# Two blocks of mixers and routed experts on one core: the order of weight places, one more place, and matmuls of two row halves issued in turn

## The chip, the core and the metric

The kernel runs on one core of one Trainium2 chip. The metric is the time of one execution on the device in microseconds (us). Engines are named as in the profile: PE is TensorE's matmuls, PEld its weight loads, DVE is VectorE, ACT is ScalarE, POOL is GpSimd, SP is SyncE, whose queue issues nearly all the transfers.

## What is computed

256 tokens of width 1024 go through two layers of a first block and one layer of a second block, all in float32.

- A layer of the first block: RMS norm; a projection to queries, keys, values and gates; "dilated" attention (4 heads, each a mixture over strides 1, 4 and 16) beside windowed attention (16 query heads, 4 key heads, a sink logit); two branch projections, gated and summed; an output projection. Then expert-choice feed-forward: each of 16 experts takes its 32 best tokens, computes `silu(a) * u` with two 1024 x 1024 weights and goes through a third.
- The second block: sine positions, a modulated norm, and a token mixer of two branches. HGRN2 is a scan with a state per head, run in both directions in 8 chunks of 32 tokens, `S_new = exp(total) * S + (k * decay)^T v`; the Hyena branch is a long convolution by DFT. Then 32 experts in 4 groups (each token goes to 2), and a last norm.

All weights are read once, some 746 MB, in chunks of 128 partitions x 2048 float32 (1 MB).

## The kernel before, in words

**Places.** SBUF holds a chunk in a *place*. There are two kinds, 9 of tag "W" and 12 of tag "T" (`PLACES`, L297). The T places are also those of the large tiles: every tag in `WHOLE` (L294) is turned into "T" by `Core.t` (L75), so activations and weights share them. `Core.use` (L51) sets a ring of tags, as `ROOM` (L296), and `Core.chunk` (L60) takes the next tag of the ring, makes a tile of it and has `fetch` (L55) load it. `fetch` chains every load behind the one before on SP's queue, so the loads start in the order of the program, and one whose place is not yet free holds up all behind it. Smaller tags have slots of their own (`SMALL`, L299): "P" and "PT" four of 128 x 512 each, "wh" and "wl" three each for the two parts, a rounded one and the rest, into which `split` (L95) divides a weight for the projections (three matmuls per product, L121 to L123).

**Order of work.** `body` (L1549) writes the program in one line: mixer, experts, mixer, experts, token mixer, mixture of experts. Inside a stage generators are interleaved by `weave` (L313). A planner (`schedule_with_timeline_sim=True`) then sets the order on each engine and gives out the slots of each tag when the program is built; the engines run their instructions in that order.

**Experts of the first block.** `experts` (L717) routes the tokens, then takes the ring `ROOM` and asks for its 19 chunks ahead of the first matmul (L793, L794), then goes over to the ring "WT" in layer 0 (where the next layer's projections, `Ahead`, are woven into the second half) or `FEW` in layer 1 (L795). Expert by expert, eight chunks each, it multiplies (L810); the gather of the tokens (`gather_x`, L889) is interleaved with expert 0, and a second gather comes before expert 2. `gs` and `sg` are its work tiles (L818, tag "P"; L824, tag "PT"). The second half goes four experts at a time over the down weights (L863), q = 0 to 3. In layer 1 the filters and the context of the second block (`prep`) are interleaved.

**Attention.** `dilated_scores` (L439) computes for one pair of heads and one half of the tokens two banks of scores (tag "sc", 2 banks): first the three matmuls (L447) of the head in partitions 0 to 63, then those of the head in 64 to 127. Each half gets a tile P (tag "P") that is masked (L414), exponentiated (L417), scaled and transposed (L434).

**Scan.** In `hgrn` (L1166) each of the 8 steps multiplies the state (L1228); the update of the state goes direction by direction (L1232 to L1247): four matmuls over 32 partitions (L1238) into a bank, then four instructions on DVE (L1245) that make the next state.

**Other users of "P".** `rstd` (L163) squares into it; `ada_gate` (L621) loads a bias `gb` into it (L632, L633), in the token mixer just ahead of the load of the first `w2z` chunk, and in `moe` (L1348) just ahead of the first 16 chunks of the last stage (`ROOM2`, L1428, L1429); the token mixer's last addition uses it for `t1` (L1314).

**Last stage.** `moe` (L1329) asks for 16 chunks in the ring `ROOM2`, then uses "WWTWT"; `moe_quad` (L1470) takes four experts at a time.

Of the kernel before, what the change touches and what calls it, by code (L numbers as in the profile page):

```python
# [2 lines left out]

# [1 line left out]

# [4 lines left out]
F = mybir.dt.float32  # L10
# [3 lines left out]
OP = mybir.AluOpType  # L14
# [3 lines left out]
T, D = 256, 1024  # L18
# [4 lines left out]
PW = 2048  # L23
BIG = -1e33
HG = 4
# [7 lines left out]
class Core:  # L33
    def __init__(self, ctx, tc, A):
        self.tc, self.nc, self.A = tc, tc.nc, A
        self.const = ctx.enter_context(tc.tile_pool(name="const", bufs=1))
        self.sb = ctx.enter_context(tc.tile_pool(name="sb", bufs=1))
        self.ps = ctx.enter_context(tc.tile_pool(name="ps", bufs=1, space=PSUM))
        self.flip = self.nsplit = self.nchunk = 0

        self.share = 4
        self.after = nullcontext
        self.idle, self.pre, self.sent = (), [], None
        self.use("W")

    def load(self, name, shape, dt=F):
# [1 line left out]
        self.fetch(t, name)  # L48
        return t

    def use(self, places):  # L51

        self.ring = cycle(places)

    def fetch(self, out, src):  # L55

# [3 lines left out]
    def chunk(self, src, parts=1):  # L60

        tag = next(self.ring)
        t = self.sb.tile([128, PW], F, name="w", tag=tag, bufs=PLACES[tag])
        n = src.shape[1] // parts
        for i in range(parts):
            self.fetch(t[:, i * n:(i + 1) * n], src[:, i * n:(i + 1) * n])
        return t

    def next_chunk(self, src, parts=1):
        return self.pre.pop(0) if self.pre else self.chunk(src, parts)  # L70
# [3 lines left out]

    def t(self, shape, name, bufs=1, tag=None, dt=F):  # L75
        tag = tag or name
        if tag in WHOLE:
            tag, bufs = "T", PLACES["T"]
        return self.sb.tile(shape, dt, name=name, tag=tag, bufs=bufs)
# [122 lines left out]
class Quarters:  # L202

    shape = (128, PW)
# [87 lines left out]
HEAD = ((1, 3), (0, 3))  # L292

WHOLE = {"x", "hTa", "hTb", "qa", "qb", "qc", "V", "G", "hgw", "hn", "ob"}  # L294
ROOM2 = "TWWTTTTWWTTTWWWW"
ROOM, FEW = "TWWWWTTTTTTWWTTTWWW", "WWWWTWWWWWT"  # L296
PLACES = {"W": 9, "T": 12}  # L297
NP = 4
SMALL = {"P": NP, "PT": NP, "wh": 3, "wl": 3, "oa": 2}  # L299
BANKS = {"mm": 2, "sc": 2, "tp": 2, "acc": 2}  # L300
# [21 lines left out]

def mixer(K, h, l, ada, first=None, ahead=None):
    nc, A = K.nc, K.A
    if ahead:
        x = ahead.x
        ahead.turned(3)
    else:
        w_in = iter(A["w_in"])

        K.idle = range(K.nsplit + HEAD[l][0], K.nsplit + HEAD[l][1])
        x = K.pair("hT")
        K.transposed(h, lambda kb, p: K.split_to(x[0][:, kb, :], x[1][:, kb, :], p, K.gmix[:, l, kb:kb + 1]),
                     banks=("tp", "sc"))

    rs = K.rstd(h)
    p = K.bank("tp")
# [101 lines left out]
    def dilated_scores(pair, tt):  # L439
        q = slice(tt * 128, tt * 128 + 128)  # L440
        Ps, m, den = [], K.t([128, 2, 3], "m3", 2), K.t([128, 4], "den", 3)
        for half in range(2):
            s, hh = 2 * pair + half, slice(half * 64, half * 64 + 64)
            p = K.bank("sc")
            for g, (o, ks) in enumerate(((0, slice(0, 256)), (256, q), (384, q))):
                b = (4 * g + s) // 2
                nc.tensor.matmul(p[:, o:o + ks.stop - ks.start], lhsT=qd[b][hh, q], rhs=qd[6 + b][hh, ks],  # L447
                                 start=True, stop=True)
            P = K.t([128, 512], "P", NP)
            mh = m[:, half]  # L450
            ttr(P[:, :256], p[:, :256], K.negd[:, 512 + tt * 256:768 + tt * 256], SLOPE_A[s], 1e30, mh[:, 0:1])
            ttr(P[:, 256:384], p[:, 256:384], K.negd[:, 1024:1152], SLOPE_A[4 + s], mh[:, 0:1], mh[:, 1:2])
            ttr(P[:, 384:], p[:, 384:], K.negd[:, 1152:1280], SLOPE_A[8 + s], mh[:, 1:2], mh[:, 2:3])
            exponential(P, mh[:, 2:3], den[:, half:half + 1])
            Ps.append(P)
        r = K.t([128, 4], "r", 3)
        nc.vector.reciprocal(r[:, :2], den[:, :2])
        for half in range(2):
            nc.vector.tensor_scalar(Ps[half], Ps[half], r[:, half:half + 1], None, op0=OP.mult)
        return pair, tt, Ps  # L460
# [160 lines left out]
def ada_gate(K, g):  # L621

    nc = K.nc
    p = K.bank("acc")
    for c in range(4):
        w = K.chunk(K.A["ada"][2, 4 * g + c])
        with K.after():
            for j in range(4):
                nc.tensor.matmul(p[32 * j:32 * j + 32, :], lhsT=K.cs32[:, 2 * c + j // 2, :],
                                 rhs=w[:, j * 512:(j + 1) * 512], start=(c == 0), stop=(c == 3),  # L630
                                 tile_position=(0, 32 * j))
    gb = K.t([128, 512], "gb", NP, tag="P")  # L632
    K.fetch(gb, K.A["gtb"][g])  # L633
    K.ms = K.t([128, 512], "ms", tag="wr")
    nc.vector.tensor_add(K.ms, p, gb)
# [81 lines left out]
def experts(K, h, l, mix, ada, prep, ahead=None):  # L717
# [4 lines left out]
    next(rt)  # L722
    for _ in mix:
        next(rt)
    q = K.logits
    rs = K.rstd(h, dve=False, tag="oa")
    lg = K.t([128, 2, NE], "lg")
# [64 lines left out]

    K.use(ROOM)  # L793
    ws = [K.chunk(A["w_eg"][l, i // KD, i % KD]) for i in range(len(ROOM))]  # L794
    K.use("WT" if ahead else FEW)  # L795
    hid, Ge = [], []
    gw = K.t([128, 4], "gw4")
    for e in range(NE):
# [16 lines left out]
                pass  # L815
        if e % 8 == 0:
            hid.append(K.t([128, 8, 4, 64], "hid", tag=own[e // 8]))
        gs = K.t([128, 512], "gs", NP, tag="P")  # L818
        K.copy(gs, gu)
        p = K.bank("tp")  # L820
        for fb in range(4):
# [209 lines left out]

def token_mixer(K, h):
    nc, A, tc = K.nc, K.A, K.tc

    sc = K.t([128, 2, D], "sincos", tag="V")
    K.fetch(sc, "sincos")
# [129 lines left out]
    def hgrn():  # L1166
# [55 lines left out]
        for n in range(8):  # L1222

            for hd in range(HG):
                for d in range(2):
                    c = 7 - n if d else n
                    tt, cc = divmod(c, 4)
                    nc.tensor.matmul(oo[tt][32 * cc:32 * cc + 32, hd * 128:(hd + 1) * 128],  # L1228
                                     lhsT=steps[d][0][:, hd, c * 32:(c + 1) * 32], rhs=S[d][:, hd * 128:(hd + 1) * 128],
                                     start=False, stop=(n >= 4 and n % 4 == 3 and hd == HG - 1),  # L1230
                                     tile_position=(0, 32 * cc), skip_group_check=True)
            for d in range(2 if n < 7 else 0):  # L1232
                wk, b, kT, end = steps[d]
                c = 7 - n if d else n
                tt, cc = divmod(c, 4)
                u = K.bank("sc")
                for hd in range(HG):
                    nc.tensor.matmul(u[:, hd * 128:(hd + 1) * 128],  # L1238
                                     lhsT=kT[32 * cc:32 * cc + 32, tt, hd * 128:(hd + 1) * 128],
                                     rhs=v[32 * cc:32 * cc + 32, tt, hd * 128:(hd + 1) * 128], start=True, stop=True,  # L1240
                                     tile_position=(32 * cc, 0))
                S2 = K.t([128, 512], "PT", NP)
                for hd in range(HG):
                    sl = slice(hd * 128, (hd + 1) * 128)
                    nc.vector.scalar_tensor_tensor(S2[:, sl], S[d][:, sl], b[:, hd, c * 32 + end:c * 32 + end + 1],  # L1245
                                                   u[:, sl], op0=OP.mult, op1=OP.add)
                S[d] = S2  # L1247
            yield

    ya = K.t([128, 2, 4, T], "ya", tag="ob", dt=FR)  # L1250
# [78 lines left out]
def moe(K, h, mix):  # L1329
# [12 lines left out]
    next(rt)  # L1342
    for _ in mix:
        next(rt)
    q = K.logits
    rs = K.rstd(h, dve=False, tag="oa")
    K.after = lambda: tc.issue_after(K.routed.ins)
# [79 lines left out]

    K.use(ROOM2)  # L1428
    K.pre = [K.chunk(A["w2eg"][2 * i + x, c]) for i in range(2) for c in range(4) for x in range(2)]  # L1429
    K.use("WWTWT")  # L1430

    def gate(*args):
        spread_gate(*args)
# [36 lines left out]
def moe_quad(K, h, xT, oh, cmb, e, i, gate):  # L1470
# [45 lines left out]
    for hf in range(2):  # L1516
        sl = slice(hf * 512, (hf + 1) * 512)
        dn = K.bank("acc")
        end = e + 4 + hf == NE2 + 1

        wd = [K.next_chunk(A["w2ed"][e + x, hf], 4 if end and x == 3 else 1) for x in range(4)]
        for c in range(4):
            for x in range(4):
                nc.tensor.matmul(dn[32 * x:32 * x + 32, :], lhsT=hid[x][:, c, :], rhs=wd[x][:, c * 512:(c + 1) * 512],  # L1524
                                 start=(c == 0), stop=(c == 3), tile_position=(0, 32 * x))
        y = K.t([128, 512], "yt", NP, tag="P")
        nc.vector.scalar_tensor_tensor(y, dn, gw, K.gt[:, 1, sl], op0=OP.mult, op1=OP.mult)
        hi, lo = yd[:, 0, sl], yd[:, 1, sl]
        K.split_to(hi, lo, y)
        for tt in range(2):  # L1530
            p = K.bank("sc")
            for n, part_ in enumerate((hi, lo)):
                nc.tensor.matmul(p, lhsT=Ge[:, tt * 128:(tt + 1) * 128], rhs=part_, start=(n == 0), stop=(n == 1))
            hs = h[:, tt, sl]
            nc.vector.tensor_add(hs, p, hs)
# [214 lines left out]
```

## Time and profile before

| | us |
|---|---|
| median of 3 runs (2227.25 to 2230.5) | 2229.97 |
| the profiled execution, its own time | 2231.4 |
| its span, first to last instruction | 2229.6 |
| PE busy | 1803.5 (81%) |
| PEld busy | 1017.9 |
| DVE busy | 761.1 |
| ACT busy | 600.3 |
| POOL busy | 222.2 |

The transfers moved 748.83 MB, 336 GB/s over the span. Busy time is what an engine's instructions cover; an engine that waits is not busy. The stretch from 0 to about 275 us is the mixer of layer 0, to 785 its experts, to 965 the mixer of layer 1, to 1455 its experts, to 1755 the token mixer, to 2210 the last experts. The rows further down give for a stretch the busy time of each engine with the number of instructions in brackets, then the clock granted to TensorE as a share of 2.4 GHz, the share of time for which the DMA engines were busy, and GB/s.

### The profile page before, as it was taken

To read this page: it belongs to the slowest core of one execution; us is meant where nothing else is said; L and a number is where in the kernel's file an instruction comes from. 1 tells how busy PE (TensorE), PEld (TensorE's weight loads), DVE (VectorE), ACT (ScalarE), POOL (GpSimd) and SP (SyncE) were. 2 spreads that over 40 slices of the span, in tenths; PEclk is the share of its full clock that TensorE was granted. 3 is DMA by queue.
4 is the path that set the end of the run, shared out by engine and by line. 5 is a ranking of instruction groups with operands and counts; after the bars stand their busy time and mean duration, and the time that the engine had idled before them with its cause. 6 is when DMAs were issued, how large, how long until landed. Compare 5 with 4: busy or idle time off the path is not lost.

```text
span 2229.6 us, 30070 instructions
## 1 busy us (share of the span) xinstructions
PE 1803.5 (81%) x12172; PEld 1017.9 (46%) x12172; DVE 761.1 (34%) x1696; ACT 600.3 (27%) x1191; POOL 222.2 (10%) x183
## 2 busy tenths in 40 slices
PE   8999996666699998987788666789999867676765
PEld 8888631110277776841234123368888412121211
DVE  5666510000045588532111111157557311111112
ACT  4666410000033357620125100055245200000000
POOL 2111200000011122300000000033134000000000
PEclk9999997777799999997799778889999999999998
DMA  8445779999999953569999999984223999999996
GB/s 342 149 146 207 313 311 420 422 421 421 421 418 419 414 210 151 216 264 399 420 420 420 421 419 420 418 337 156 76 70 149 418 420 421 420 421 421 421 421 284
DMA packets 108442, 748.83 MB, mean 336 GB/s; under 512 B 14120, under 2 KB 14537, under 8 KB 18697
## 3 DMA queue, kind: packets, MB, share of 16 engines
q1 hardware_dynamic: 107752, 745.79, 82.3%
q8 instruction: 98, 1.61, 0.3%
q10 hardware_dynamic: 544, 1.05, 0.1%
q14 instruction: 48, 0.39, 0.1%
HBM read 745.74 MB, written 1.05 MB: 335 GB/s over the span
## 4 chain that ended last, share of the span: by engine, by line
PE 40%; DMA 29%; issue 22%; DVE 6%; ACT 2%; POOL 0%; POOLq 0%; SPq 0%; ACTq 0%; DVEq 0%
DMA w<-in_w_eg 18%; DMA w<-in_w_ed 9%; PE mm L121 7%; PE mm L122 6%; PE mm L123 6%; PE acc L863 4%; PE mm L810 3%; PE sc L889 2%; DVE wl L102 1%; PE acc L518 1%; DMA w<-in_w2z 1%; PE acc L949 1%; PE acc L1228 1%; DMA cx<-in_ctx 1%; PE sc L122 1%
## 5 line engine op out<-in xcount | busy, mean ns | idle before, releaser
L810 PE MATMUL mm<-w,xT 128*32 128x512 f32 x2048 | 327.8, 743 | 116.6 <-DMA w<-in_w_eg 116.2
L101 ACT ACTIVATE wh<-w 128x512 fp32r<-128x512 f32 x384 | 239.9, 630 | 290.5 <-PE mm L122 218.0
L121 PE MATMUL mm<-hTa,wh 128*128 128x256 f32 x960 | 281.0, 294 | 5.6 <-DVE Ga L245 1.7
L123 PE MATMUL mm<-hTa,wl 128*128 128x256 f32 x960 | 274.2, 288 | 1.9 <-DVE wl L102 1.6
L122 PE MATMUL mm<-hTb,wh 128*128 128x256 f32 x960 | 272.5, 285 | 2.2 <-DVE hTb L113 1.6
L102 DVE TENSOR_TENSOR wl<-w,wh 128x512 fp32r<-128x512 f32 x286 | 220.1, 775 | 108.9 <-ACT wh L101 106.1
L1485 PE MATMUL mm<-w,xT 128*32 128x512 f32 x1024 | 176.9, 613 | 71.9 <-DMA w<-in_w2eg 71.4
L863 PE MATMUL acc<-w,hid 128*32 128x256 f32 x2048 | 184.7, 449 | 62.3 <-DMA w<-in_w_ed 62.3
L102 POOL TENSOR_TENSOR wl<-w,wh 128x512 fp32r<-128x512 f32 x98 | 129.0, 1317 | 901.9 <-ACT wh L101 803.9
L810 PEld LDWEIGHTS mm<-w,xT 128*32 128x32 f32 x2048 | 51.3, 120 | 329.6 <-DMA w<-in_w_eg 271.6
L121 PEld LDWEIGHTS mm<-hTa,wh 128*128 128x128 f32 x960 | 181.8, 190 | 28.4 <-issue 15.7
L123 PEld LDWEIGHTS mm<-hTa,wl 128*128 128x128 f32 x960 | 181.0, 190 | 10.6 <-issue 3.4
L122 PEld LDWEIGHTS mm<-hTb,wh 128*128 128x128 f32 x960 | 182.0, 190 | 6.2 <-issue 2.4
L863 PEld LDWEIGHTS acc<-w,hid 128*32 128x32 f32 x2048 | 80.5, 128 | 148.6 <-DMA w<-in_w_ed 83.1
L1524 PE MATMUL acc<-w,work 128*32 128x512 f32 x512 | 94.9, 640 | 32.9 <-DMA w<-in_w2ed 32.9
L1485 PEld LDWEIGHTS mm<-w,xT 128*32 128x32 f32 x1024 | 34.2, 110 | 189.1 <-DMA w<-in_w2eg 140.8
L178 POOL TENSOR_TENSOR rs<-rs,mhalf 128x2 f32<-128x2 f32 x9 | 6.8, 751 | 1008.4 <-DVE rs L177 1008.4
L826 DVE TENSOR_TENSOR hid<-tp,sg 128x256 f32<-128x256 f32 x32 | 13.6, 425 | 216.8 <-ACT sg L825 216.8
L113 DVE SCALAR_TENSOR_TENSOR yd<-acc,gw,yd 128x256 fp32r<-128x256 f32 x32 | 15.5, 483 | 181.2 <-ACT yd L112 181.2
L112 ACT ACTIVATE yd<-acc,gw 128x256 fp32r<-128x256 f32 x32 | 15.2, 475 | 220.0 <-PE acc L863 220.0
L91 DVE COPY gs<-mm 128x512 f32<-128x512 f32 x16 | 11.1, 692 | 181.5 <-PE mm L810 181.5
L825 ACT ACTIVATE sg<-tp 128x256 f32<-128x256 f32 x32 | 12.3, 384 | 218.3 <-PE tp L822 218.3
(468 smaller groups left out, 2471.8 us busy)
## 6 DMA issues: line engine op xcount, KB each, us to landing
w<-in_w_eg SPq DMA_DIRECT2D x256, 1024.0 KB, 19.8
w<-in_w_ed SPq DMA_DIRECT2D x128, 1024.0 KB, 18.5
w<-in_w2eg SPq DMA_DIRECT2D x128, 1024.0 KB, 19.8
w<-in_w2ed SPq DMA_DIRECT2D x63, 1024.0 KB, 19.8
w<-in_ada SPq DMA_DIRECT2D x24, 1024.0 KB, 11.7
w<-in_w_in SPq DMA_DIRECT2D x22, 1024.0 KB, 7.2
w<-in_wk SPq DMA_DIRECT2D x20, 1024.0 KB, 17.7
w<-in_w_b SPq DMA_DIRECT2D x8, 1024.0 KB, 6.0
```

The lines of the kernel that those rows point to most:

```text
L101: self.hi = nc.scalar.activation(hi, src, AF.Copy)
L102: (nc.gpsimd if n in self.idle or n % self.share == self.share - 1 else nc.vector).tensor_tensor(lo, src, hi.bitcast(F), OP.subtract)
L121: mm(out, lhsT=l[0], rhs=r[0], start=start, stop=False)
L122: mm(out, lhsT=l[0], rhs=r[1], start=False, stop=False)
L123: mm(out, lhsT=l[1], rhs=r[0], start=False, stop=stop)
L518: nc.tensor.matmul(po[half * 64:half * 64 + 64, :T], lhsT=V[:, kt, c:c + 64], rhs=PTs[half][:, kt * 256:(kt + 1) * 256], start=(kt == 0), ...
L810: nc.tensor.matmul(gu[32 * j:32 * j + 32, :], lhsT=xT[:, k, (e % 8) * CAP:(e % 8 + 1) * CAP], rhs=w[:, j * 512:(j + 1) * 512], start=(k == ...
L863: nc.tensor.matmul(dn[32 * x:32 * x + 32, :T], lhsT=hid[e // 8][:, e % 8, f, hh * 32:hh * 32 + 32], rhs=ws[x][:, fb * T:(fb + 1) * T], sta ...
L889: nc.tensor.matmul(p[:, :T], lhsT=hn[:, tt, kb * 128:(kb + 1) * 128], rhs=oh[:, tt].rearrange("p a b -> p (a b)"), start=(tt == 0), stop=( ...
L949: nc.tensor.matmul(p[:, :T], lhsT=w[:, o:o + 128], rhs=cT[:, k, :], start=(k == 0), stop=(k == KD - 1))
L1485: nc.tensor.matmul(gu[o:o + 32, :], lhsT=xT[:, k, y:y + CAP2], rhs=ws[x][:, (2 * kk + j) * 512:(2 * kk + j + 1) * 512], start=(k == 0), st ...
L1524: nc.tensor.matmul(dn[32 * x:32 * x + 32, :], lhsT=hid[x][:, c, :], rhs=wd[x][:, c * 512:(c + 1) * 512], start=(c == 0), stop=(c == 3), ti ...
```

## The change

One T place more (13), and no slots of their own for tag "P": the four P tiles are now quarters of one T place that a stage takes at its first P and drops at its end (`held`). The tiles `gb`, `gs` and `yt` move from "P" to "PT". The rings ahead of the three expert stages get two chunks more: they begin with a second T, and one chunk ("Q") goes as four quarters into three "wh" and one "wl" slot. The rings used after them (`AGAIN`, `AGAIN2`) repeat the first ring's order without its first two T and without Q. The matmuls of the dilated scores and of the state updates alternate between the two row halves or the two directions.

```diff
+    def use(self, places, first=""):
+        self.ring = chain(first, cycle(places))
...
     def chunk(self, src, parts=1):
         tag = next(self.ring)
+        if tag == "Q":
+            return self.quarters(src, ("wh", "wh", "wh", "wl"))
...
+    def quarters(self, src, tags):
+        ts = []
+        for i, tag in enumerate(tags):
+            ts.append(self.sb.tile([128, 512], F, name="w4", tag=tag, bufs=SMALL[tag]))
+            self.fetch(ts[-1], src[:, i * 512:(i + 1) * 512])
+        return Quarters(ts)
...
     def t(self, shape, name, bufs=1, tag=None, dt=F):
         tag = tag or name
+        if tag == "P":
+            if self.held is None:
+                self.held = self.sb.tile([128, PW], F, name="P4", tag="T", bufs=PLACES["T"]), cycle(range(0, PW, 512))
+            o = next(self.held[1])
+            return self.held[0][:, o:o + shape[1]]
...
-ROOM2 = "TWWTTTTWWTTTWWWW"
-ROOM, FEW = "TWWWWTTTTTTWWTTTWWW", "WWWWTWWWWWT"
-PLACES = {"W": 9, "T": 12}
+AGAIN, AGAIN2 = "WWWWTTTTTTWWTTTWWW", "WWTTTTWWTTTWWWW"
+ROOM2 = "TTWWTTTTWWTTQTWWWW"
+ROOM, FEW = "TTWWWWTTTTTTWWTTQTWWW", "WWWWTWWWWWT"
+PLACES = {"W": 9, "T": 13}
...
@@ mixer, token_mixer (at the start), experts, moe (after the mixer's last step)
+    K.held = None
...
@@ dilated_scores
+        ps = [K.bank("sc") for _ in range(2)]
+        for g, (o, ks) in enumerate(((0, slice(0, 256)), (256, q), (384, q))):
+            for half in range(2):
+                hh, b = slice(half * 64, half * 64 + 64), 2 * g + pair
+                nc.tensor.matmul(ps[half][:, o:o + ks.stop - ks.start], lhsT=qd[b][hh, q], rhs=qd[6 + b][hh, ks],
+                                 start=True, stop=True)
         for half in range(2):
-            s, hh = 2 * pair + half, slice(half * 64, half * 64 + 64)
-            p = K.bank("sc")
-            for g, (o, ks) in enumerate(((0, slice(0, 256)), (256, q), (384, q))):
-                b = (4 * g + s) // 2
-                nc.tensor.matmul(p[:, o:o + ks.stop - ks.start], lhsT=qd[b][hh, q], rhs=qd[6 + b][hh, ks],
-                                 start=True, stop=True)
+            s, p = 2 * pair + half, ps[half]
...
@@ ada_gate, experts, moe_quad
-    gb = K.t([128, 512], "gb", NP, tag="P")
+    gb = K.t([128, 512], "gb", NP, tag="PT")
-        gs = K.t([128, 512], "gs", NP, tag="P")
+        gs = K.t([128, 512], "gs", NP, tag="PT")
-        y = K.t([128, 512], "yt", NP, tag="P")
+        y = K.t([128, 512], "yt", NP, tag="PT")
...
@@ experts
-    K.use("WT" if ahead else FEW)
+    K.use(AGAIN if ahead else FEW, AGAIN)
...
@@ hgrn
+            if n < 7:
+                us = [K.bank("sc") for _ in range(2)]
+                at = [divmod(7 - n if d else n, 4) for d in range(2)]
                 for hd in range(HG):
+                    for d in range(2):
+                        tt, cc = at[d]
+                        kT = steps[d][2]
+                        nc.tensor.matmul(us[d][:, hd * 128:(hd + 1) * 128],
+                                         lhsT=kT[32 * cc:32 * cc + 32, tt, hd * 128:(hd + 1) * 128],
+                                         rhs=v[32 * cc:32 * cc + 32, tt, hd * 128:(hd + 1) * 128], start=True, stop=True,
+                                         tile_position=(32 * cc, 0))
...
@@ moe
     K.use(ROOM2)
     K.pre = [K.chunk(A["w2eg"][2 * i + x, c]) for i in range(2) for c in range(4) for x in range(2)]
-    K.use("WWTWT")
+    K.pre += [K.chunk(A["w2ed"][x, 0]) for x in range(len(ROOM2) - 16)]
+    K.use(AGAIN2)
```

## Rows read from the trace of the kernel before

**Rows 1.** Busy time by stage: us, busy of each engine, PEclk, DMA share, GB/s
```profile
75.00:200.00 125.00, 125.00 (x934) 103.54 (x934) 83.90 (x265) 78.71 (x191) 15.53 (x12) 1.00 0.39 137
300.00:620.00 320.00, 213.79 (x1342) 50.22 (x1346) 19.14 (x37) 15.40 (x33) 0.00 (x0) 0.78 1.01 421
620.00:785.00 165.00, 165.00 (x1547) 127.21 (x1540) 86.79 (x136) 56.60 (x99) 23.46 (x19) 1.00 1.01 415
800.00:890.00 90.00, 82.94 (x569) 61.51 (x568) 83.50 (x256) 61.97 (x162) 24.18 (x17) 1.00 0.42 153
1025.00:1450.00 425.00, 314.75 (x2154) 125.74 (x2157) 62.73 (x145) 76.83 (x117) 0.70 (x1) 0.82 1.01 418
1475.00:1700.00 225.00, 217.76 (x1594) 193.81 (x1595) 132.46 (x237) 106.25 (x198) 72.69 (x56) 0.99 0.41 152
1755.00:2205.00 450.00, 317.25 (x1798) 92.00 (x1797) 67.04 (x137) 32.18 (x60) 0.00 (x0) 0.97 1.01 421
```

**Rows 2.** Layer 0, 207 to 300 us: timelines (start, us), one issue's landing
```profile
207.21 63.46 SPq L58 DMA_DIRECT2D w<-in_w_eg  x19
...
294.30 0.33 SPq L58 DMA_DIRECT2D w<-in_w_eg  x1
...
w<-in_w_eg SPq DMA_DIRECT2D x1, 1024.0 KB, 4.7
...
284.94 1.06 PE L810 MATMUL mm<-w,xT 128*32 128x512 f32 x8
...
287.00 1.07 PE L810 MATMUL mm<-w,xT 128*32 128x512 f32 x8
```

**Rows 3.** Layer 1, 970 to 1003 us: timelines of SP's queue and of PE
```profile
972.93 0.33 SPq L58 DMA_DIRECT2D w<-in_w_eg  x1
...
1002.71 0.33 SPq L58 DMA_DIRECT2D w<-in_w_eg  x1
...
973.86 1.06 PE L810 MATMUL mm<-w,xT 128*32 128x512 f32 x8
```

**Rows 4.** Before the last stage: SP's timeline and its wait (total, times, longest), PE
```profile
1684.75 2.85 SPq L58 DMA_DIRECT2D w<-in_ada  x4
1726.09 0.33 SPq L58 DMA_DIRECT2D gb<-in_gtb  x1
...
SPq L58 <- POOL h L1317: 18.8, 1, 18.8
...
1745.93 3.64 PE L629 MATMUL acc<-w,cs 128*32 128x512 f32 x32
...
1762.19 1.07 PE L1485 MATMUL mm<-w,xT 128*32 128x512 f32 x8
```

**Rows 5.** Start of the token mixer: SP's wait and issue, DVE and PE timelines
```profile
SPq L58 <- ACT sq L174: 10.2, 1, 10.2
...
1460.78 0.33 SPq L58 DMA_DIRECT2D gb<-in_gtb  x1
...
1472.64 1.09 DVE L1052 TENSOR_TENSOR hTb<-ht,hTa 128x256 fp32r<-128x256 f32 x3
...
1468.44 0.58 PE L121 MATMUL mm<-hTa,wh 128*128 128x256 f32 x1
```

**Rows 6.** Dilated scores (L447) and state updates (L1238): PE busy, PEld busy; timeline
```profile
70.00:110.00 40.00, 8.35 (x48) 6.39 (x48) 1.00 0.37 132
...
73.30 0.48 PE L447 MATMUL sc<-qa 64*128 64x256 f32 x1
...
74.58 0.48 PE L447 MATMUL sc<-qb,qa 64*128 64x128 f32 x2
...
1550.00:1630.00 80.00, 16.37 (x112) 12.17 (x112) 1.00 0.23 80
```

**Rows 7.** One line's instructions (L417, ns min/median/max) and ACT's timeline
```profile
L417 ACT ACTIVATE P<-P,m x80: 492/506/725, 78.4 to 890.6; 128x256 f32<-128x256 f32 x64, 128x512 f32<-128x512 f32 x16
...
289.17 0.47 ACT L89 ACTIVATE xT<-sc,gffn 128x256 f32<-128x256 f32 x1 [4.43 <-PE sc L889]
```

More of the change, by code (lines that the diff above doesn't have):

```diff
@@ L1 @@
 from contextlib import ExitStack, nullcontext
-from itertools import cycle, islice
+from itertools import chain, cycle, islice
 import numpy as np
@@ L42, in __init__ @@
         self.after = nullcontext
-        self.idle, self.pre, self.sent = (), [], None
+        self.idle, self.pre, self.sent, self.held = (), [], None, None
         self.use("W")
@@ L49, in load @@
         return t
-    def use(self, places):
-        self.ring = cycle(places)
+    def use(self, places, first=""):
+        self.ring = chain(first, cycle(places))
     def fetch(self, out, src):
@@ L724, in experts @@
         next(rt)
+    K.held = None
     q = K.logits
@@ L1033, in token_mixer @@
     nc, A, tc = K.nc, K.A, K.tc
+    K.held = None
     sc = K.t([128, 2, D], "sincos", tag="V")
@@ L1231, in hgrn @@
                                      tile_position=(0, 32 * cc), skip_group_check=True)
[L1232 to L1236, printed above, removed]
-                for hd in range(HG):
[L1238 to L1247, printed above, removed]
+            if n < 7:
+                us = [K.bank("sc") for _ in range(2)]
+                at = [divmod(7 - n if d else n, 4) for d in range(2)]
+                for hd in range(HG):
+                    for d in range(2):
[5 more added lines that the diff above has]
+                                         tile_position=(32 * cc, 0))
+                for d in range(2):
+                    b, end = steps[d][1], steps[d][3]
+                    c = 7 - n if d else n
+                    S2 = K.t([128, 512], "PT", NP)
+                    for hd in range(HG):
+                        sl = slice(hd * 128, (hd + 1) * 128)
+                        nc.vector.scalar_tensor_tensor(S2[:, sl], S[d][:, sl], b[:, hd, c * 32 + end:c * 32 + end + 1],
+                                                       us[d][:, sl], op0=OP.mult, op1=OP.add)
+                    S[d] = S2
             yield
@@ L1344, in moe @@
         next(rt)
+    K.held = None
     q = K.logits
```

## The prediction

> **What bounds the kernel now.** I read the page's 40 slices first: the DMA engines are full in three long blocks and mostly idle between them. The table by stage [rows 1] shows why. In 300 to 620, 1025 to 1450 and 1755 to 2205 us the DMA share is 1.01 at some 420 GB/s while PE is busy for only about 70% of the time: these expert stages end when their bytes are in. A chunk of 1 MB (1.0486e6 bytes) at 421 GB/s takes 2.49 us, and that is the price of every chunk below. Between the blocks PE is the bound (all 125 us of 75 to 200, all 165 of 620 to 785, 217.8 of 225 in the token mixer) or DVE (83.5 of 90 us in layer 1's mixer). So an expert stage can end earlier only if its queue of loads becomes unbroken earlier; the second view is therefore SP's queue at the head of each block.
>
> Layer 0 [rows 2]: 19 chunks go out from 207 to 271 us, then the queue stands. One load goes alone after that, landing 4.7 us after its issue, and the unbroken run begins at 294.30, each after a wait for an L810 matmul, that is, for a place to be read out. Layer 1 [rows 3]: after its 19 the queue crawls through seven loads from 972.93 on and is unbroken from 1002.71. Last stage [rows 4]: the queue has nothing to do from 1687.6 (the four `ada` loads) to 1726.09, where `gb` goes out after waits of which the last, 18.8 us, is for POOL's addition at L1317; the 16 chunks stand behind it. That addition reads the P tile of the token mixer's first `t1`, four P tiles before `gb` in the program. The same shows at 1460.78 [rows 5]: `gb` waits for the first square of the second `rstd`, again four P tiles before. From these two I take that a tag's slots are given out in the program's order, the one that is free first going first; the terms below rest on it.
>
> **The change part by part.** *Layer 0.* `ROOM` now lists 21 chunks, its first T places go to the tiles made after experts 0 and 1 (`hid`, the second `xT`), and `AGAIN` asks for places in the order in which experts read them out. So the first refill needs the third chunk read: L810 at 284.94 ends at 286.0 [rows 2]. PE reads the next one 2.06 us later (287.00), and so on, faster than 2.49, so the run is unbroken from there. Chunk 22 then lands at 286.0 + 4.7 = 290.7. Before, chunk 21 opened the run at 294.30, so chunk 22 landed at 294.3 + 4.7 + 2.5 = 301.5. Gain 10.8 us. The two added chunks themselves land by 271 + 4.7 + 2 x 2.5 = 281, ahead of the refill. In 620 to 785, where PE and DMA are both full [rows 1], both start 10.8 us earlier, so nothing is given back.
> *Layer 1.* The third chunk is read at 973.86 + 1.06 = 974.9 [rows 3]; chunk 22 lands at 979.6 and chunk 27 at 979.6 + 5 x 2.49 = 992.1. Before, chunk 27 (19 + 7 + 1) went out at 1002.71 and landed at 1007.4. Gain 15.3 us; `prep`'s small loads come after in both. Together these two lie between 5 us each (two more chunks and no better order) and 12 and 17.
> *Last stage.* `gb` takes a PT slot, whose earlier users are done by then, and goes at 1687.6; the 18 chunks follow as T places fall free (the ring's T places are the gate, branch, product and `w2o` tiles and the P quarter). The last four need `ada`'s places, read out by L629 until 1749.6 [rows 4]: all 18 are in by 1749.6 + 2.2 + 4 x 2.49 = 1761.8. Refills need the third and fourth chunk, read until 1763.26: chunk 19 lands at 1768.0. Before it landed at 1726.5 + 4.7 + 18 x 2.49 + 1.2 (the `gfin` load) = 1777.2. Gain 9.2, with 6 if the first T is free only at 1721, and 11 if `gfin` falls into a gap.
> *Token mixer.* Here `gb` on PT costs. Ahead of it in the program stand eight `ht` tiles on four PT slots, so it waits for the fifth, read by L1052, whose last blocks run from 1472.64 [rows 5]; without splits in between I put it at 1470.5. The queue's `w2z` loads go 9.7 us later, PE's first product moves from 1468.44 to about 1477. PE was still waiting for `hTb` in part of that time, so I take 6.5 of 8.5; the ends are 0 and 11. Cover there is none: PE is nearly full from 1475 on [rows 1].
> *Matmuls.* The eight halves of layer 0 take 8.35 us of a full PE [rows 6]. In one place the two halves already overlap: the second half's first matmul starts at 73.30, inside the first half's run. At full overlap half the time, 4.2, is saved; the first call has part of it, so 3.5 (0 to 4.2). In layer 1 the same saving lies behind DVE [rows 1]: 1 (0 to 4). State updates: 16.37 us [rows 6], 8.2 at full overlap; the planner already sets other matmuls between them, so 5 (0 to 8.2). Both "sc" banks are now asked for at once, so the first half waits for the second's bank as well; I leave that inside the lower ends. The Trainium skill ("TensorEngine Tiling (Array Packing)", Gotcha 1) speaks against the change here: row tiles need PSUM banks of their own, so PSUM and not the array may become the limit. By it the 9.5 us of these three terms would shrink to nothing; no row prices it.
> *At nothing:* the quarters of P (a slot for four, as before), `gs` and `yt` on PT (the full DMA engines cover them; without that, 0.5 us per expert), nine more DMA issues (the queue idles there).
>
> Sum: 10.8 + 15.3 + 9.2 + 3.5 + 1 + 5 - 6.5 = 38.3 us. The profiled execution took 2231.4 (span 2229.6), 1.4 above the median of 2229.97. So 2231.4 - 38.3 - 1.4 = **2191.7 us**.
>
> **The rivals.** *`gb` in the token mixer doesn't wait* (a PT slot is free for it): 2191.7 - 6.5 = 2185.2. For it: the queue reaches `gb` before any `ht` exists; against: both waits on P went by program order. 0.09.
> *The rings don't meet the order of release*, and only the two added chunks count, 5.0 per stage: 2191.7 + 35.3 - 15 = 2212. For it: the planner's clock and not the chip's decides who gets a place. Against: T waits in rows 2 and 3 fit the program's order. 0.08.
> *Layer 0's lead is given back* where PE is full (620 to 785): 2202.5. 0.05.
> *Alternation drains the array.* A lone 128-wide matmul (two passes) holds PE for 0.48 us; the 56 of the state updates, in streams, take 16.37 / 56 = 0.29 each [rows 6]. If every matmul cost the 0.48, those of layer 0 and of the updates, 24 + 56 on a full PE, would lose 80 x 0.19 = 15.2 and the 9.5 would be gone: 2216.4. The overlap at 73.30 speaks against it. The Trainium skill has the rule beside it (same page, Key Properties): a change of tiling mode drains TensorE, a change of tile doesn't; by that this rival falls, and the trace agrees at 73.30. 0.04.
> *Slower: P's quarters are held apart no longer.* If a write to one quarter waited for the readers of the whole place, each of the 48 P tiles of the two mixers would wait for the one before: its exponential takes 0.51 us [rows 7], and scaling and transposing I put at as much again twice, 1.5 us, together 73 us: 2265. It decides from 38.3 / 48 = 0.8 us each. Against it: ACT writes one block of `xT` at 289.17 [rows 7] after L810 has read another at 284.94 [rows 2], so parts of a tile are told apart. 0.04.
> *Nothing comes of it*, since every place freed early is taken by another tile: 2230. The three standing queues speak against it. 0.03.
>
> **How the numbers follow.** The forecast keeps 0.67. The runs before spread over 3.25 us, and some 0.2% (4.5 us) is what can be told from no change. Faster by more: 0.67 + 0.09 + 0.08 + 0.05 + 0.04 = 0.93; within: 0.03; slower: 0.04. The forecast's own range is 2183 to 2203, as the ends of its seven terms don't fall together. With the first rival below and the second and third above it, 2181 to 2212 holds about 0.8.
>
> **What would show it.** Right: SP's queue unbroken from about 286 us in layer 0 and from about 975 (less what layer 0 gained) in layer 1; `gb` issued right behind the last `ada` load and no DMA gap of 38 us before the last stage; the dilated matmuls of layer 0 near 4.7 us and the state updates near 8 to 11; `gb` at the start of the token mixer waiting for DVE L1052, with PE's first `w2z` product some 8 us later behind the last expert addition. Wrong: a queue that stands on a T place ahead of free W places, PE idle inside the dilated scores, or expert stages with a DMA share below 1.

## The result and the profile after

| | us | ratio to before | 95% interval |
|---|---|---|---|
| kernel before, median | 2229.28 | | |
| changed kernel, median of 4 runs (2200.25 to 2207.07) | 2204.5 | 0.9888 | 0.987 to 0.9906 |
| the forecast | 2191.7 | | |

The change is 1.1% faster, 24.8 us where 38.3 were forecast; the time lies in the range of 2181 to 2212, but 1.5 us above the forecast's own range of 2183 to 2203. The profiled execution took 2205.3 (span 2203.5, 26.1 below the span before).

The table by stage of the changed kernel (busy time of PE, PEld, DVE, ACT, POOL with instructions; granted clock; DMA share; GB/s):

```profile
300.00:620.00 320.00, 218.54 (x1443) 59.42 (x1443) 25.39 (x46) 21.31 (x44) 2.57 (x2) 0.80 1.01 421
620.00:785.00 165.00, 162.74 (x1488) 126.03 (x1488) 91.86 (x148) 54.67 (x97) 22.85 (x19) 0.99 0.99 405
1025.00:1430.00 405.00, 293.46 (x2116) 117.54 (x2111) 55.53 (x130) 76.09 (x116) 0.70 (x1) 0.87 1.01 419
1755.00:2180.00 425.00, 306.65 (x1704) 87.94 (x1702) 65.60 (x134) 28.77 (x56) 0.00 (x0) 0.95 1.01 421
```

As in [rows 1] the expert stages run at a DMA share of 1.01 and some 420 GB/s: they are not quicker, they begin and end earlier. (The second row now ends some 13 us into the next mixer, hence its 0.99.)

So the useful view is a *lead*: the start of one and the same instruction in the trace before, less its start in the other trace, at seven places: the eighth gate product of layer 0's mixer (L569, at 210.9 us before), the 57th load of `w_ed` (736.1, end of layer 0), the 27th gate product (911.4, layer 1's mixer), the last load of `w_ed` (1431.6), the first state update on DVE (L1245, 1563.0), the first product behind the scan (L1144, 1629.0) and the last load of `w2ed` (2198.6). The gain of a stage is the lead at its end less that at its beginning.

| gain in us | forecast | changed kernel |
|---|---|---|
| layer 0 mixer (dilated scores) | +3.5 | +2.4 |
| layer 0 experts (head) | +10.8 | +11.6 |
| layer 1 mixer (dilated scores) | +1.0 | -0.3 |
| layer 1 experts (head) | +15.3 | +14.4 |
| token mixer up to the scan (`gb` on PT) | -6.5 | -7.3 |
| scan (state updates) | +5.0 | -3.6 |
| last stage | +9.2 | +8.7 |
| sum | +38.3 | +25.9 |

Of the 12.4 us missing, 8.6 are in the scan and 2.4 in the dilated scores. The rest came within 1 us. Now the views, in the order of the table.

SP's queue at the head of layer 0, of layer 1 and of the last stage, changed kernel (start, time to the end of the last issue, number of issues; the quarters of Q are single issues; the rows are cut at 300, 972 and 1700 us), then SP's waits from 1668 to 1740 us for the projections' matmuls (total, times, longest):

```profile
284.86 15.11 SPq L58 DMA_DIRECT2D w<-in_w_eg  x8
...
961.27 10.61 SPq L58 DMA_DIRECT2D w<-in_w_eg  x6
...
1672.07 0.52 SPq L58 DMA_DIRECT2D gb<-in_gtb  x1
1677.95 21.26 SPq L58 DMA_DIRECT2D w<-in_w2eg  x7
...
SPq L58 <- PE mm L139: 31.0, 3, 15.7
```

Against 294.30 [rows 2] and 1002.71 [rows 3] the queue goes on from 282.80 (one load) and 284.86, and from 961.27, with no second stop in these rows; `gb` of the last stage follows the `ada` loads directly, at 1672.07 and not at 1726.09 [rows 4]. Behind the first chunk of the last stage the queue does stand once more, 15.7 us for the second T, with W places behind it; the last experiment tries what that costs.

The start of the token mixer: SP's waits (total, times, longest), then the timeline of SP, then that of PE (in square brackets the idle time before, and what ended it):

```profile
SPq L58 <- DVE hTb L1075: 21.4, 1, 21.4
```

```profile
1443.62 0.33 SPq L58 DMA_DIRECT2D gb<-in_gtb  x1
```

```profile
1449.66 0.58 PE L137 MATMUL mm<-hTa,wh 128*128 128x256 f32 x1 [7.08 <-ACT wh L117]
1450.05 0.41 PE L138 MATMUL mm<-hTb,wh 128*128 128x256 f32 x1
```

L1075 is L1052 of before: `gb` waits 21.4 us for the reader of the fifth `ht`, as forecast, `w2z` stands behind it, and PE idles 7.08 us before its first product. In the kernel before `gb` waited 10.2 us for a square, and PE's first product came at 1468.44 [rows 5] with no such gap ahead of it.

The matmuls issued in turn, PE and PEld busy by stretch: dilated scores (L466) in both mixers, then state updates (L1263):

```profile
0.00:200.00 200.00, 7.06 (x48) 4.91 (x48) 1.00 0.55 203
785.00:965.00 180.00, 8.70 (x48) 6.32 (x48) 0.97 0.54 206
...
1530.00:1605.00 75.00, 16.32 (x112) 12.13 (x112) 0.95 0.24 85
```

Against 8.35 and 16.37 [rows 6]: 1.3 us less in layer 0, nothing to speak of in the scan, and layer 1 has the 8.70 us that it had before. The forecast wanted 4.7, and 8 to 11.

### The profile page after: what moved, and what is told of

Its sections match the earlier page's. It is cut to its first block, busy times and chain, and to the rows that moved or that the text cites. A ratio compares the mean times of both kernels' runs of the same rounds, so it can differ in the third digit from the quotient of the medians.

```text
span 2203.5 us, 30089 instructions
## 1 busy us (share of the span) xinstructions
PE 1791.7 (81%) x12172; PEld 1014.8 (46%) x12172; DVE 761.7 (35%) x1696; ACT 599.4 (27%) x1191; POOL 221.3 (10%) x183
## 4 chain that ended last, share of the span: by engine, by line
PE 40%; DMA 31%; issue 22%; DVE 6%; ACT 1%; POOL 0%; POOLq 0%; DVEq 0%; SPq 0%; ACTq 0%
DMA w<-in_w_eg 21%; DMA w<-in_w_ed 9%; PE mm L137 7%; PE mm L139 7%; PE mm L138 7%; PE acc L885 4%; PE mm L832 2%; PE sc L911 2%; DVE wl L118 1%; DMA w<-in_w2z 1%; PE acc L539 1%; PE acc L1251 1%; PE sc L138 1%; PE sc L139 1%; PE tp L453 1%
## 5 line engine op out<-in xcount | busy, mean ns | idle before, releaser
L139 PEld LDWEIGHTS mm<-hTa,wl 128*128 128x128 f32 x960 | 182.9, 192 | 12.4 <-issue 5.5
L1554 PEld LDWEIGHTS acc<-w,work 128*32 128x32 f32 x512 | 19.7, 109 | 98.5 <-DMA w<-in_w2ed 48.6
```

Of the source, the lines that this page charges most:

```text
L139: mm(out, lhsT=l[1], rhs=r[0], start=False, stop=stop)
```

## The experiments

Each run's stage gains, as in the table above, against the same trace of before. Columns: layer 0 mixer and experts, layer 1 mixer and experts, token mixer to the scan, scan, last stage; then median and ratio to the kernel before with its interval.

| run | M0 | X0 | M1 | X1 | gb | scan | last | median | ratio (95%) |
|---|---|---|---|---|---|---|---|---|---|
| changed, again | 2.0 | 10.3 | -0.4 | 14.3 | -7.1 | -0.6 | 8.8 | 2205.82 | 0.9889 (0.9872 to 0.9905) |
| `gb` on P | 2.7 | 9.8 | 0.7 | 13.9 | 0.8 | -0.6 | 10.7 | 2193.59 | 0.9829 (0.9812 to 0.9845) |
| updates undone | 2.1 | 10.3 | -0.2 | 13.8 | -6.3 | 0.0 | 8.4 | 2202.66 | 0.9876 (0.986 to 0.9893) |
| dilated undone | 0.8 | 10.1 | -0.3 | 13.5 | -6.5 | -2.1 | 10.1 | 2205.58 | 0.9883 (0.9867 to 0.99) |
| old rings | 2.7 | 6.2 | 1.8 | 1.7 | -9.7 | -0.6 | 8.0 | 2220.72 | 0.9956 (0.9942 to 0.997) |
| no extra chunks | 0.8 | 9.3 | 1.1 | 9.2 | -6.8 | -2.1 | 7.7 | 2210.93 | 0.991 (0.9893 to 0.9927) |
| before, last `gb` on PT | -0.2 | 1.0 | 0.1 | 0.1 | 0.2 | 0.0 | 6.5 | 2223.22 | 0.9968 (0.9957 to 0.998) |
| `gb` on P, updates undone | 1.6 | 12.3 | 0.0 | 14.3 | -0.1 | 0.0 | 10.9 | 2192.55 | 0.9831 (0.9814 to 0.9847) |
| before, updates in turn | 0.7 | 0.9 | 0.2 | 0.3 | 0.0 | -0.6 | 0.0 | 2231.16 | 1.0005 (0.9994 to 1.0016) |
| before, dilated in turn | 2.6 | 1.8 | 0.0 | 0.1 | 0.2 | 0.0 | 0.0 | 2227.72 | 0.9991 (0.9979 to 1.0003) |
| `gb` in a wh slot | 2.1 | 12.7 | -0.1 | 14.0 | 0.1 | 0.0 | 10.9 | 2192.58 | 0.9831 (0.9812 to 0.9851) |
| T later in the ring | 1.4 | 13.1 | -0.3 | 13.9 | 0.6 | -1.5 | 11.7 | 2191.75 | 0.9841 (0.9806 to 0.9876) |

The same code differs between rows by up to 2 us in M0 and some 3 in X0; a smaller difference between two rows is not read.

**The changed kernel, again.**

> The changed kernel unaltered, on the chip that also runs the next three. Theory (the change's gains hold and what is missing of the forecast is the clock in the scan): 2200 to 2207 us as in its four runs; in its profile the lead over the kernel before is again some 14 us after layer 0's experts, 27 after layer 1's, 20.8 at the first projections of the token mixer, and then either 20.8 or 17.2 after the scan, as the granted clock in the 20 us around the last scan steps is 1.00 or 0.83. Rival (the 3.6 us lost in the scan are caused by the new order of the matmuls): 17.2 after the scan with the clock at 1.00 all through.

2205.82 us. Up to the scan the gains are those of the changed kernel's first trace, but for 1.3 us in layer 0's experts; in the scan only 0.6 us were lost and not 3.6. The last 30 us of the scan, by granted clock (third number from the end), first the changed kernel's trace, then this one's:

```profile
1582.00:1592.00 10.00, 10.00 (x66) 7.61 (x65) 5.11 (x17) 1.75 (x3) 0.00 (x0) 0.92 0.01 2
1592.00:1602.00 10.00, 10.00 (x58) 7.59 (x58) 2.98 (x10) 1.26 (x2) 1.28 (x1) 0.84 0.29 106
1602.00:1612.00 10.00, 10.00 (x48) 6.58 (x48) 2.70 (x7) 1.89 (x3) 1.23 (x1) 0.89 0.01 2
```

```profile
1584.00:1594.00 10.00, 10.00 (x71) 7.61 (x70) 5.11 (x17) 2.38 (x4) 0.00 (x0) 1.00 0.01 2
1594.00:1604.00 10.00, 10.00 (x69) 7.27 (x68) 4.36 (x14) 1.89 (x3) 1.28 (x1) 1.00 0.28 106
1604.00:1614.00 10.00, 10.00 (x49) 6.12 (x49) 3.25 (x5) 1.13 (x2) 2.31 (x2) 1.00 0.21 75
```

PE is busy throughout in both. In the first the clock fell, to 0.92, 0.84 and 0.89; the share missing, 0.8 + 1.6 + 1.1, is 3.5 us of work at full clock (an estimate), enough for the other 3 us. So the 3.6 are two things: 0.6 that comes in all four traces with the new order and a full clock, and a clock that falls in some executions.

**The state updates undone.**

```diff
-            if n < 7:
-                us = [K.bank("sc") for _ in range(2)]
...
+            for d in range(2 if n < 7 else 0):
...
+                u = K.bank("sc")
                 for hd in range(HG):
-                    for d in range(2):
```

> The changed kernel with the state updates direction by direction again, as before. Theory (the planner had the two directions side by side on PE in the kernel before already, so the alternation is worth nothing): busy time of the update matmuls near 16.4 us as in both kernels, time within 2 us of the changed kernel in this call, but for the clock. Rival of the forecast (the alternation is worth 5 us): 2209 us. Rival (the alternation costs the 3.6 us that are lost in the scan): 2201 us, clock of that stretch 1.00.

2202.66 us, busy time 16.37 us, scan 0.0: undoing the alternation loses nothing and gives the 0.6 us back. (The median is 3.2 us lower, but the runs of the two overlap.) The order of the matmuls on PE says why. These are the update matmuls as PE's program has them (a and b are the two directions; a gap means other matmuls between), the kernel before first, then the changed one:

```
a a aa bbbbaaaa bbbb aa aabbbb a a aabbbb a a a abbbb a a a abbbb a a a abbbb
a a aa bbbbaaaa bbbb aa bbabab a a bbabab a a a bbbab a a a bbbab a a a bbbab
```

The planner has set them singly between other matmuls. In the last three steps three of direction a go ahead between the state products either way, and one stands beside b's four either way; only that one changes its place. What the new order does is to put it behind three of b's, and DVE's next state of a waits for it. The fifth step, PE's last group of updates and DVE's start (behind PE), kernel before, then changed again:

```profile
1600.22 1.16 PE L1238 MATMUL sc<-vt,z 32*128 32x128 f32 x10
1600.74 2.16 DVE L1245 SCALAR_TENSOR_TENSOR PT<-PT,z,sc 128x128 f32<-128x128 f32 x8 [4.48 <-PE sc L1238]
...
1582.22 1.15 PE L1263 MATMUL sc<-vt,z 32*128 32x128 f32 x10
1583.21 2.16 DVE L1273 SCALAR_TENSOR_TENSOR PT<-PT,z,sc 128x128 f32<-128x128 f32 x8 [3.31 <-PE sc L1263]
```

DVE starts 0.99 us after the group and not 0.52. DVE's updates from the second step on (first and last start), kernel before, changed again, updates undone, and before with updates in turn:

```profile
L1245 DVE SCALAR_TENSOR_TENSOR PT<-PT,z,sc x48: 339/343/348, 1572.3 to 1618.4; 128x128 f32<-128x128 f32 x48
```

```profile
L1273 DVE SCALAR_TENSOR_TENSOR PT<-PT,z,sc x48: 340/343/348, 1553.2 to 1602.5; 128x128 f32<-128x128 f32 x48
```

```profile
L1268 DVE SCALAR_TENSOR_TENSOR PT<-PT,z,sc x48: 337/342/348, 1552.7 to 1598.7; 128x128 f32<-128x128 f32 x48
```

```profile
L1250 DVE SCALAR_TENSOR_TENSOR PT<-PT,z,sc x48: 336/340/349, 1570.2 to 1619.6; 128x128 f32<-128x128 f32 x48
```

From first to last start it is 46.1 and 46.0 us in the old order, 49.3 and 49.4 in the new one: the chain of states takes 3.2 us longer. PE is busy throughout, and of the 3.2 us only 0.6 are left behind the scan; that PE does projections in the meantime that it would do later fits this, but was not counted.

**The updates in turn, in the kernel before.** The opposite edit, alone.

> The kernel before with the state updates alternating between the two directions, and nothing else. Theory (the planner interleaves the directions either way; alternated, the scan's last step ends 3 to 4 us later and most of it comes back in the projections behind it): busy time of the updates 16.3 us, lead lost by the end of the token mixer 0.6 us, with the clock at 1.00 in the last 40 us of the scan; 2 to 3.6 us where the clock falls there. 2231 to 2234 us. Rival of the forecast: 2226 us.

2231.16 us, ratio 1.0005 (0.9994 to 1.0016): no change clear of noise; busy time 16.32 us, scan -0.6 at a clock of 1.00. The forecast's rival of 2226 falls.

**The dilated scores undone.**

```diff
-        ps = [K.bank("sc") for _ in range(2)]
-        for g, (o, ks) in enumerate(((0, slice(0, 256)), (256, q), (384, q))):
-            for half in range(2):
...
         for half in range(2):
-            s, p = 2 * pair + half, ps[half]
+            s, hh = 2 * pair + half, slice(half * 64, half * 64 + 64)
+            p = K.bank("sc")
+            for g, (o, ks) in enumerate(((0, slice(0, 256)), (256, q), (384, q))):
```

> The changed kernel with the dilated scores head by head again. Theory (the alternation is worth the 1.8 us by which the lead grows from 0.6 to 2.4 us in the first 105 us of layer 0, and nothing in layer 1): busy time of these matmuls back to 8.35 us in layer 0, 2206.3 us. Rival of the forecast (4.5 us over both layers): 2209 us. Rival (the 1.8 us come from elsewhere): no change, 2204.5 us.

The busy time in layer 0 is back to 8.35 us. The lead behind the mixer is 0.8; over the ten traces with the scores in turn it is 2.0 in the mean (0.8 to 2.7), over the three without 0.4 (-0.2 to 0.8). The total, 2205.58, does not tell it apart, as the other stages vary by more.

**The dilated scores in turn, in the kernel before.**

> The kernel before with the dilated scores alternating between the two halves, and nothing else. Theory (1.3 us less busy time in layer 0, nothing in layer 1): lead of some 1.3 us at the end of layer 0's mixer, 2229.7 us. Rival of the forecast: 4.5 us, 2226.5 us. Rival (nothing): 2231 us.

2227.72 us, 0.9991 (0.9979 to 1.0003): 7.06 us busy in layer 0, 8.70 in layer 1, lead 2.6 behind layer 0's mixer and nothing more in layer 1's. That agrees with 1.3 us less of busy time; the total alone would not show it. The changed kernel's timeline shows where the overlap is had, and a last row, of the kernel before, that layer 1 had one such place already:

```profile
78.27 0.70 PE L466 MATMUL sc<-qa 64*128 64x256 f32 x2
78.81 0.60 PE L466 MATMUL sc<-qb,qa 64*128 64x128 f32 x4
79.66 0.70 PE L466 MATMUL sc<-qa 64*128 64x256 f32 x2
80.19 0.60 PE L466 MATMUL sc<-qb,qa 64*128 64x128 f32 x4
85.11 0.70 PE L466 MATMUL sc<-qa 64*128 64x256 f32 x4
87.49 0.71 PE L466 MATMUL sc<-qb,qa 64*128 64x128 f32 x8
...
802.73 0.70 PE L447 MATMUL sc<-qa 64*128 64x256 f32 x4
```

At 85.11 both halves go in turn and take 0.70 us together, as one alone at 78.27 (each matmul has two rows here). The array does what the change hopes for. But the call at 78.27 is issued half by half all the same, as before. Two of layer 0's four calls changed their order on PE, and none of layer 1's: one of its four goes in turn, and that one did so in the kernel before (802.73).

**`gb` of the token mixer on P.**

```diff
-    gb = K.t([128, 512], "gb", NP, tag="PT")
+    gb = K.t([128, 512], "gb", NP, tag="PT" if g else "P")
```

> The changed kernel, with the bias tile of the token mixer back on tag P (now a quarter of the held place), the one of the last stage left on PT. Theory (on PT it waits for the transposed tiles ahead of it, and with it the loads of w2z): the bias goes out at some 1433 us behind a square of the second norm as in the kernel before, PE's first w2z product comes 6 to 7 us earlier, 2198 us. Rival (PE waits for the last transposed tile at that point anyway, the loads' 10 us hide): 2204 us. Third (a quarter of the held place is free later than a slot of its own): slower than 2204.

2193.59 us, 12.2 below the changed kernel's 2205.82. SP's wait and PE's start:

```profile
SPq L58 <- ACT P L190: 10.3, 1, 10.3
```

```profile
1440.55 1.11 PE L209 MATMUL tp<-ident,hn 128*128 128x128 f32 x4 [0.79 <-ACT ht L1073]
1441.31 0.56 PE L137 MATMUL mm<-hTa,wh 128*128 128x256 f32 x1
1441.67 0.41 PE L138 MATMUL mm<-hTb,wh 128*128 128x256 f32 x1
```

The first product comes at 1441.31 and not at 1449.66, with no idle time before it: +0.8 in place of -7.1 us. Another 1.9 us come in the last stage, for a reason that was not followed; together 9.8, the difference of the two profiled spans (2201.9 and 2192.1; that of the changed kernel is its quickest run). The rival that PE waits for the transposed tiles anyway falls, and so does the one that a quarter of the held place comes later.

**`gb` in a slot of its own kind.** The same with the updates undone and `gb` under tag "wh".

> The changed kernel with the updates direction by direction and the token mixer's bias in a slot of tag wh, which is free at that time, so that neither a square nor a transposed tile holds it. Theory (behind the bias the loads of w2z go out at some 1425 us, 9 us before those of the run with the bias on P, but PE's first product waits for the first transposed tiles at 1441 us): the same as that run within 2 us, 2190.5 to 2192.5 us. Rival (the projections of the token mixer are still held by their loads): some 5 us faster, 2187 us. Rival (a wh slot held by the bias stalls the splits): slower, 2196 us.

2192.58 us. `gb` goes out at 1422.71, 11 us earlier still, and gains nothing: PE's first product waits for the transposed tiles. On P the wait is already hidden.

**The old rings behind the longer heads.**

```diff
-    K.use(AGAIN if ahead else FEW, AGAIN)
+    K.use("WT" if ahead else FEW)
...
-    K.use(AGAIN2)
+    K.use("WWTWT")
```

> The changed kernel with the two more chunks, but after them the rings of the kernel before (WT, FEW, WWTWT) in place of the order of release. Theory (both parts count): a T asked for second waits until the seventh chunk of the head is read, so the queue stands again for some 5 us in layer 0, 7 in layer 1, 3 in the last stage: 2204.5 + 15 = 2220 us. Rival (only the two more chunks count): 2204.5 us. Rival (only the order counts): 2238 us, i.e. the heads' gain of 34 us gone.

2220.72 us, as expected. SP's waits in 974 to 998 us (layer 1), then its timeline on both sides of the stop in layer 0:

```profile
SPq L58 <- PE mm L832: 20.7, 5, 14.0
```

```profile
281.77 0.33 SPq L58 DMA_DIRECT2D w<-in_w_eg  x1
...
290.00 2.88 SPq L58 DMA_DIRECT2D w<-in_w_eg  x4
```

The queue stands 8.2 us after the first refill in layer 0, for a T while W places fall free, and 14.0 us in layer 1, for a W while T places do. The two more chunks alone leave 6.2 us in layer 0 and 1.7 in layer 1. Why the token mixer stands at -9.7 here and not at some -7 was not followed.

**The order of release without the extra chunks.**

```diff
-ROOM2 = "TTWWTTTTWWTTQTWWWW"
-ROOM, FEW = "TTWWWWTTTTTTWWTTQTWWW", "WWWWTWWWWWT"
+ROOM2 = "TWWTTTTWWTTTWWWW"
+ROOM, FEW = "TWWWWTTTTTTWWTTTWWW", "WWWWTWWWWWT"
```

> The changed kernel with the order of release, but only 19, 19 and 16 chunks ahead (no second T, no Q). Theory (two chunks are two times 2.49 us in each stage): 2204.5 + 15 = 2219.5 us. Rival (the chunks ahead only wait longer in their places, the order alone makes the queue unbroken): 2204.5 us.

2210.93 us, a miss of my theory: the extra chunks are worth some 5 us and not 15. By stage it is 5.1 in layer 1; the 1 or so in layer 0 and in the last stage is no more than the same code varies by. One reason can be read from the traces: with a second T ahead, the first refill waits for the third chunk to be read and not for the second. In layer 0 it goes out 6.0 us after PE's first product of the stage (276.77 and 282.80, changed kernel) and not 3.2 us after it (277.88 and 281.07, this run), which takes back 2.8 of the 5 us. In layer 1 the same shift is 1.8 us (5.2 after 3.4); why 5.1 are left there was not followed.

**The last stage's `gb` on PT, in the kernel before.**

```diff
-    gb = K.t([128, 512], "gb", NP, tag="P")
+    gb = K.t([128, 512], "gb", NP, tag="PT" if g else "P")
```

> The kernel before with one edit: the bias tile of the last stage on PT, the one of the token mixer stays on P. Theory (the queue of the last stage starts at 1688 and not at 1726 us, then it is the last four places that count): the gap without transfers goes, the 17th chunk lands some 6 us earlier, 2231.3 - 6 = 2225 us. Rival (the places, not the bias, hold the chunks): 2231 us. Rival (all of the last stage's 9 us come from this tile): 2222 us.

2223.22 us: 6.5 of the last stage's 8.7 us are this one tile; ring, place and chunks together add 2.

**Both mends at once**: `gb` of the token mixer on P, updates undone.

> The changed kernel with the token mixer's bias on P and the state updates direction by direction. Theory (the two are independent, and the alternation of the updates costs 0 to 3 us by a later end of the scan): 2190 to 2193.6 us, the scan's lead kept whole. Rival (the updates' alternation is worth something once the projections come earlier): over 2194.5 us.

2192.55 us, ratio 0.9831 (0.9814 to 0.9847), the scan's lead kept whole. It is faster than both kernels, 12 to 13 us faster than the changed one; against `gb` on P alone the 1 us less is not clear of the spread.

**The second T of the last ring two places later**, on top of that.

```diff
-ROOM2 = "TTWWTTTTWWTTQTWWWW"
+ROOM2 = "TWWTTTTTWWTTQTWWWW"
```

> As the run with the bias on P and the updates direction by direction, and in the last stage's ring the second T moved behind the first two W, because it waits 15.7 us there with free W places behind it. Theory (the last places of the head, which come free with the reading of the ada chunks, and the start of the reading set the end of the head): within 1.5 us of 2192.5 us. Rival (each chunk that goes out earlier is 2.49 us): 2187.5 us.

2191.75 us, the same (one of its four runs took 2203.78). Two chunks go out ahead of the wait, and nothing comes of it: the wait of 15.7 us in that queue costs nothing that shows here. It was expected so, as the last four places and the first reading set the end of the head. In this trace the scan lost 1.5 us with the updates in their old order, the clock at 0.88 and 0.95 in 20 us of it: a falling clock there does not need the new order.

## Why the prediction was right or wrong

**Direction and bound: right.** The expert stages hold their 420 GB/s, and the lead at the last load, 25.9 us, is nearly all of the 26.1 by which the span fell. That the time lies in the stated range is in part luck: at 2204.5 it is outside the forecast's own 2183 to 2203, and the room up to 2212 was there for two rivals, rings that miss the order and a lead given back, neither of which came true.

**Slots in program order: right.** That was the premise of most terms, and the token mixer shows it most sharply: `gb` waited for the fifth `ht`'s reader, named beforehand. The rival that it doesn't wait falls. Forecast -6.5, measured -7.3 and -7.1; PE had no cover there, as the run with `gb` on P shows, which stands at +0.8.

**Heads: right in sum.** 10.8 and 15.3 against 11.6 and 14.4. How the parts add up was not forecast: chunks alone 6.2 and 1.7, order alone 9.3 and 9.2, both 10.3 to 11.6 and 14.3. The rival of rings that miss the order put the chunks at 5 per stage, 2212; the run of that case took 2220.72. Layer 0's lead was not given back between 620 and 785: it is 14.0 us at 736.1 and 13.7 at 911.4.

**Last stage: right in size** (9.2 against 8.7), with `gb` the larger part. One of the signs of being wrong did show, a queue that stands on a T ahead of W places, 15.7 us; moving that T changed nothing.

**State updates: wrong, the step that failed.** "8.2 at full overlap; the planner already sets other matmuls between them, so 5 (0 to 8.2)". I took 5 of the 8.2 us as if the order in the program were the order on PE. There the planner had most of a's matmuls spread out among others, so that in either order one or two of four stand beside b's, and the edit moved only these, the wrong way for the chain through DVE. Measured: busy time 16.32 after 16.37, a loss of 0.6 us, and in the changed kernel's profile another 3 by the clock. The range of that term should have reached below nothing.

**Dilated scores: mechanism right, size wrong.** 4.5 for both layers; measured some 1.3, as the edit reached PE in two of eight calls, both in layer 0; the other six kept their order, one of them, in layer 1, in turn already. Both halves do overlap, as the rows at 85.11 show: the rival of a drained array falls. The Trainium skill ("TensorEngine Tiling (Array Packing)", Key Properties) says that a change of tiling mode drains the engine and a mere change of tile does not; on the second the trace agrees, with 0.70 us for both halves. The prediction took what the Trainium skill says of PSUM banks (same page, Gotcha 1) to put the three terms of 9.5 us at nothing, and that is close to what came. But no row shows a bank as the reason: PE is 10.00 of 10.00 us busy in the scan, and the same two banks carry the calls that overlap.

**P's quarters: right.** With the dilated scores undone, layer 0's mixer stands at +0.8 us with P as quarters of one place; the slower rival wanted tens of us lost. P's place by itself was not tried, nor were `gs` and `yt` on PT, which the prediction put at nothing.

## What to carry to other kernels

Where a planner orders the engines, an edit of the program's order is a hint: read the order that each engine gets, before and after, and price only the instructions that change their place, together with who waits for the last of them. A tile that moves to another tag inherits that tag's queue of users: list the tiles ahead of it in the program, and what stands behind its load. When the order of refills is that of release, the number of chunks ahead counts for less than it seems.

## What had not been expected

PE's 7.08 us without work before 1449.66 cost more than themselves. The products behind them take 0.41 us each until 1453.8 and 0.28 from then on, as the granted clock (third number from the end) goes from 0.50 to 0.98, from the lower to the upper of TensorE's two levels, 1.2 and 2.4 GHz:

```profile
1449.60:1453.80 4.20, 4.13 (x18) 3.91 (x19) 1.90 (x3) 1.68 (x4) 0.38 (x1) 0.50 1.01 425
1453.80:1458.00 4.20, 4.20 (x35) 4.03 (x35) 0.69 (x1) 2.98 (x5) 1.49 (x2) 0.98 1.01 423
```

With `gb` on P, without the gap, the products started at the lower level too, but took 0.41 us for some 2 us only, so the gap costs some 1 us on top (an estimate: 2 us more at half the clock lose 1 us of work).

And the clock fell in the middle of the scan, with PE busy without a gap, in four of the fourteen traces, at a price of 1.5 to 3 us. What sets it off stays open: it fell in three of seven traces with the updates in turn and in one of seven without.
